# A decay chain behind each projection, a stacked low-rank product, earlier masks and ScalarE evictions in a two-layer backbone step

## The chip, the cores and the metric

The kernel runs on one core of a Trainium2 chip as one program. The metric is the device time of one execution in microseconds; lower is better. The time of a kernel is the median of several executions. One more execution is taken with the hardware profiler, and all rows below are from that one.

## What is computed

One inference step of a backbone with two layers, for 128 context tokens and 1024 latent tokens (1152 columns in all), width 1024, in f32. The change lies in the first (even) layer, ahead of its attention. Cut to what matters:

```
def even_project(h, w_in):                       # h: normalized and modulated tokens
    qa, ka, va, qb, kb, vb, rb, lr = split_cols(h @ w_in, SIZES_EVEN)

def gla_bidir(q, k, v, lr, w_alpha, b_alpha, s0_f, s0_b):
    la = log_sigmoid(einsum('btzr,zrk->btzk', lr, w_alpha) + b_alpha) / 16     # rank 16, two directions
    ...                                          # chunks of 64 tokens
    bcum = cumsum(ac, axis=3)                    # running sum of the log decay inside a chunk
    attn = where(mask, einsum('nbhid,nbhjd->nbhij', q * exp(bcum), k * exp(-bcum)), 0)

def latent_attention(q, k, v, kc, vc, sink): ... # windowed attention with a sink; q and k rotated first
```

So each layer-0 token gets attention queries, keys and values, queries, keys and values of a gated linear attention with four heads, and 32 low-rank numbers `lr`. A product of `lr` with `w_alpha`, a log-sigmoid and a running sum give one decay array per head, 128 rows (64 forward, 64 backward) by 1152 columns.

## The kernel before

Everything is held transposed: features on the 128 partitions, tokens along the free dimension, in three chunks of 384 columns (`CW`, `NCH`). Products are made at f32 accuracy from rounded halves: `hi` is the value rounded to f32r, `lo` the rest, and `mm3` (lines 147 to 150) issues hi*hi, hi*lo and lo*hi, three passes of TensorE. A plain f32 product is issued as two passes.

SBUF is cut into one-buffer slots, `us(i)` (lines 84 to 90): a tile named for slot i takes the slot when the earlier tile of that slot has been read for the last time. Slots 32 and 33 are two halves of one double tile (`up(32)`). PSUM has three `mm` banks (`mmps`, line 105), two `S`, two `X` and one `O` (`aux`). Small rings of SBUF buffers hold temporaries: `t` (5), `ta` (3), `raw` (3) and `w` (4, two weight pairs). The order of instructions on each engine is set when the kernel is built: a planner takes, in a simulated run, the instruction that comes first in the program among those that are ready. A later line can therefore run ahead of an earlier one.

The stages around the change, in program order:

- Slots 16 to 23 hold the input X[0] to X[7]. The first chunk is normalized into the halves H (slots 0 to 15).
- **The token-row product** (lines 605 to 623). For each of nine blocks of 128 tokens and for two column halves, 24 passes give 128 tokens by 272 columns: values `vb` of the linear attention (512 columns in all) and, at the end of the second half, the 32 columns of `lr`. The second and third chunk are normalized in between, at blocks 2 and 5 (line 607), in place in X. Each result leaves PSUM by a copy into a `ta` buffer (line 620, ScalarE for the first half and VectorE for the second), is stored to `d_vb`, and the 32 columns are copied to `lrs3` (line 623, VectorE, slot 32).
- Nine transposes and three copies turn `lrs3` into `lrt`, 32 rows by 1152 (lines 625 to 631, slot 33). `RM` (slot 23) is a mask of ones with a zero at each chunk start; `walp` (slot 22) holds the low-rank weights.
- **gla_pre(hd)** (lines 641 to 655), called for the four heads one after the other: the low-rank product in three chunks (line 647, f32, 32 rows deep), a copy with bias into `et` (line 648, ScalarE), minimum (649), Exp (650), Ln (651), subtraction (652) and the two running sums as scans (653, 654) into `bt`, which goes to `d_b` in DRAM. `et` is slot 31, `bt` slot 30. This is called a decay chain below.
- **Projections.** `proj` takes one weight unit over three chunks, 24 passes each: keys KA (unit 4), rotated by `rope` (lines 664 to 670: a shuffle, two products, one on GpSimd, and a sum); values VST (unit 5); the cached and own keys and values are split into halves; then queries 0 to 3 (lines 720 to 724), each evicted by ScalarE (line 674), rotated and stored to `d_qa`.
- Nine attention blocks, a further projection and two modulation units (`ada_unit`) between each, and behind the last block `gla_init`, which loads the masks `mq` and `m2` (lines 855 to 858), and `gla_a(0)`. Then the linear attention, the output projection, the feed-forward part and the second layer. None of these is edited except `gla_init`.

## Time and profile before

| | us |
|---|---|
| median of 3 runs | 2837.32 (2836.78 to 2839.9) |
| profiled execution | 2838.03 |
| its span, first to last instruction | 2836.3 |
| TensorE busy | 2685.5 (95%) |
| VectorE busy | 2056.6 (73%) |
| ScalarE busy | 1310.2 (46%) |
| GpSimd busy | 1321.5 (47%) |
| mean granted TensorE clock | 0.960 |

PE is TensorE, PEld its weight loads, DVE VectorE, ACT ScalarE, POOL GpSimd, SP SyncE. A busy share is an average over the whole span; for one stage the tables by stage count. The granted clock is the part of 2.4 GHz that TensorE had; 0.50 is its lower level of 1.2 GHz. A wait is put down to what ended last before the engine went on. The end of a matmul is modelled, so neighbouring passes overlap in the rows: the distance of their starts is their cost. Lines 139, 140, 144, 145 and 148 to 150 are helpers that many stages use.

### The profile page before, as it was taken

The numbers are of one execution on the slowest core, as the hardware profiler recorded it, in microseconds if no ns is written. First come the engines' busy times: TensorE is split into PE (matmuls) and PEld (weight loads), VectorE is DVE, ScalarE is ACT, GpSimd is POOL, SyncE is SP. The second block draws the span as 40 slices with busy tenths as digits, with TensorE's granted clock in tenths as the row PEclk, the third lists the DMA queues.
The fourth block names the chain that finished last, engine by engine and source line by source line (L and its number), as shares of the span: only waits on it lengthen the run. The fifth ranks groups of instructions, "written<-read, shape, count | busy, mean of one in ns | idle before, by whom it ended". The sixth has DMA issues, their size and how long they took to land. (4 is left out here: it accounts for less than half of the span.)

```text
span 2836.3 us, 48190 instructions
## 1 busy us (share of the span) xinstructions
PE 2685.5 (95%) x18540; PEld 2549.1 (90%) x18540; DVE 2056.6 (73%) x3544; ACT 1310.2 (46%) x2369; POOL 1321.5 (47%) x783
## 2 busy tenths in 40 slices
PE   6999996888999999999999899989899999999998
PEld 4888884666999999999999899989899999999998
DVE  5466667653588878778777768866888787778876
ACT  5345556434543444435334365564634434443433
POOL 4230104322565555456555536543555555455453
PEclk8999997879999999999999999999999999999999
DMA  8125347643153222622323223453433224433322
GB/s 283 58 85 175 125 140 248 196 147 123 61 208 97 83 90 86 229 88 85 102 83 116 73 75 125 137 164 105 160 131 92 89 89 129 156 96 106 99 83 71
DMA packets 134661, 346.55 MB, mean 122 GB/s; under 512 B 14336, under 2 KB 60416, under 8 KB 134432
## 3 DMA queue, kind: packets, MB, share of 16 engines
q1 hardware_dynamic: 134432, 343.48, 37.1%
q8 instruction: 146, 2.39, 0.3%
q14 instruction: 83, 0.68, 0.1%
HBM read 282.66 MB, written 60.76 MB: 121 GB/s over the span
## 5 line engine op out<-in xcount | busy, mean ns | idle before, releaser
L150 PE MATMUL mm<-u,w 128*128 128x384 f32 (+1 forms) x1324 | 423.9, 322 | 4.2 <-POOL w L140 4.2
L148 PE MATMUL mm<-u,w 128*128 128x384 f32 (+1 forms) x1241 | 401.4, 324 | 4.7 <-DMA u<-d_yg 3.1
L149 PE MATMUL mm<-u,w 128*128 128x384 f32 (+1 forms) x1241 | 398.7, 322 | 3.2 <-POOL u L145 3.2
L140 POOL TENSOR_TENSOR w<-raw,w 128x1024 fp32r<-128x1024 f32 (+1 forms) x67 | 149.1, 2226 | 359.6 <-ACT w L139 299.8
L150 PEld LDWEIGHTS mm<-u,w 128*128 128x128 f32 x1324 | 252.9, 191 | 9.1 <-POOL w L140 4.7
L148 PEld LDWEIGHTS mm<-u,w 128*128 128x128 f32 x1241 | 238.1, 192 | 13.7 <-issue 9.0
L149 PEld LDWEIGHTS mm<-u,w 128*128 128x128 f32 x1241 | 238.1, 192 | 4.9 <-POOL u L145 3.4
L317 DVE SCALAR_TENSOR_TENSOR u<-mm,mods,u 128x288 f32<-128x288 f32 (+4 forms) x345 | 145.4, 451 | 86.2 <-PE mm L150 79.6
L150 PE MATMUL mm<-u,u 128*128 128x288 f32 (+1 forms) x672 | 198.4, 297 | 0.2 <-POOL u L445 0.2
L150 PE MATMUL X<-u,w 128*128 128x288 f32 (+1 forms) x644 | 196.7, 307 | 0.0
L148 PE MATMUL mm<-u,u 128*128 128x288 f32 (+1 forms) x606 | 180.3, 298 | 5.5 <-ACT u L394 3.7
L149 PE MATMUL mm<-u,u 128*128 128x288 f32 (+1 forms) x606 | 180.0, 297 | 0.4 <-POOL u L395 0.3
L148 PE MATMUL X<-u,w 128*128 128x288 f32 (+1 forms) x577 | 175.1, 305 | 2.4 <-DVE u L145 2.4
L149 PE MATMUL X<-u,w 128*128 128x288 f32 (+1 forms) x577 | 175.2, 304 | 1.1 <-DVE u L278 1.1
L148 PE MATMUL S<-u,w 128*128 128x288 f32 (+1 forms) x526 | 161.8, 308 | 10.0 <-ACT t L1178 3.8
L149 PE MATMUL S<-u,w 128*128 128x288 f32 (+1 forms) x526 | 161.1, 306 | 3.0 <-DVE u L1149 3.0
L148 PE MATMUL mm<-u,c 128*128 128x288 f32 (+2 forms) x497 | 153.1, 308 | 0.7 <-DVE ta L505 0.7
L149 PE MATMUL mm<-u,c 128*128 128x288 f32 (+2 forms) x497 | 152.0, 306 | 0.0
L451 POOL TENSOR_TENSOR u<-raw 128x512 f32<-128x512 f32 x82 | 135.8, 1656 | 32.6 <-DMA raw<-in_w_fi_dram 16.4
L447 DVE TENSOR_TENSOR u<-u,raw 128x512 f32<-128x512 f32 x82 | 142.0, 1731 | 0.8
L148 PE MATMUL X<-u,u 128*128 128x288 f32 x433 | 128.6, 297 | 1.5 <-ACT u L449 0.6
L149 PE MATMUL X<-u,u 128*128 128x288 f32 x433 | 128.3, 296 | 0.2
(450 smaller groups left out, 9133.6 us busy)
## 6 DMA issues: line engine op xcount, KB each, us to landing
raw<-in_w_fi_dram SPq DMA_DIRECT2D x164, 512.0 KB, 3.6
raw<-in_w_fo_dram SPq DMA_DIRECT2D x96, 384.0 KB, 3.1
raw<-in_w_ada_dram SPq DMA_DIRECT2D x48, 512.0 KB, 4.8
c<-in_w_ada_dram SPq DMA_DIRECT2D x32, 512.0 KB, 5.4
d_w<-u SPq DMA_DIRECT2D x20, 512.0 KB, 3.6
u<-d_w SPq DMA_DIRECT2D x20, 512.0 KB, 4.9
u<-in_w_ada_dram SPq DMA_DIRECT2D x16, 512.0 KB, 10.3
raw<-in_w_fo_dram SPq DMA_DIRECT2D x16, 512.0 KB, 4.1
```

Source lines behind the costliest of these rows:

```text
L140: gp.tensor_tensor(out=lo[:, :n], in0=raw[:, :n], in1=f_(hi[:, :n]), op=ALU.subtract)
L148: pe.matmul(ps, wh, hh, start=first, stop=False)
L149: pe.matmul(ps, wh, hl, start=False, stop=False)
L150: pe.matmul(ps, wl, hh, start=False, stop=last)
L317: ve.scalar_tensor_tensor(x, ps[:, s0:s1], mod(l, j, cond, n), x, op0=ALU.mult, op1=ALU.add)
L447: ve.tensor_tensor(out=s2, in0=s1, in1=a11, op=ALU.subtract)
L451: gp.tensor_tensor(out=s3, in0=a11, in1=a21, op=ALU.subtract)
```

## The change

1. `lrs3` moves from slot 32 to slot 21. Both halves of each token-row result, and the 32 columns, are copied out by ScalarE.
2. `lrt` becomes an f32r tile of 96 rows in the left half of the double slot 32: rows 0 to 31 and 32 to 63 the rounded half, written by two ScalarE copies, rows 64 to 95 the rest, by one VectorE subtraction. `walp` is stacked to match (rounded, rest, rounded), made from the loaded weights `wa` (slot 20). Line 647 becomes one f32r product 96 rows deep, the sum of the three partial products.
3. The four chains are no longer called in a row: `gla_pre(0)` follows the key projection, `gla_pre(1)` to `gla_pre(3)` follow the projections of queries 0 to 2. Queries 0 and 1 are projected, rotated and stored ahead of the splits of keys and values, query 2 is projected ahead of them and rotated behind them, query 3 stays behind. The slots of the query tiles change accordingly (21, 28, 21, 22).
4. The load and the two copies of the masks move from `gla_init` to ahead of the rotation tables.

```diff
-        lrs3 = us(32)[:, :288].rearrange("p (b n) -> p b n", b=9)
+        lrs3 = us(21)[:, :288].rearrange("p (b n) -> p b n", b=9)
...
-                (sc.copy if hf == 0 else ve.tensor_copy)(s, ps[:, :n])
+                sc.copy(s, ps[:, :n])
                 sy.dma_start(out=d_vb[blk][:, hf * 272:hf * 272 + n], in_=s)
                 if hf == 1:
-                    ve.tensor_copy(lrs3[:, blk], ps[:, 240:272])
-
-        lrt = us(33)[0:32]
+                    sc.copy(lrs3[:, blk], ps[:, 240:272])
+
+        lrt = up(32, F32R)[:, :U]
         for b0, b1 in ((0, 4), (4, 8), (8, 9)):
...
-            ve.tensor_copy(lrt[:, b0 * 128:b1 * 128], ps[0:32, :n])
+            g = slice(b0 * 128, b1 * 128)
+            for q in range(2):
+                sc.copy(lrt[q * 32:q * 32 + 32, g], ps[0:32, :n])
+            ve.tensor_tensor(out=lrt[64:96, g], in0=ps[0:32, :n], in1=f_(lrt[0:32, g]), op=ALU.subtract)
...
-        walp = us(22)[0:32, :512].rearrange("p (h n) -> p h n", h=4)
-        sy.dma_start(out=walp, in_=A["w_alp"])
+        walp = us(22, F32R)[:, :512]
+        wa = us(20)[0:32, :512]
+        sy.dma_start(out=wa.rearrange("p (h n) -> p h n", h=4), in_=A["w_alp"])
+        for q in range(2):
+            sc.copy(walp[q * 64:q * 64 + 32], wa)
+        ve.tensor_tensor(out=walp[32:64], in0=wa, in1=f_(walp[0:32]), op=ALU.subtract)
...
-                pe.matmul(ps[:, :CW], walp[:, hd], lrt[:, ch(c)], start=True, stop=True)
+                pe.matmul(ps[:, :CW], walp[0:96, hd * 128:hd * 128 + 128], lrt[0:96, ch(c)], start=True, stop=True)
...
-        for hd in range(4):
-            gla_pre(hd)
-
+        mqf = tmpa(384)
+        sy.dma_start(out=mqf, in_=A["gmask"])
+        ve.tensor_copy(mq.rearrange("p a b -> p (a b)"), mqf[:, :256])
+        ve.tensor_copy(m2, mqf[:, 256:])
...
-        KA, VST = us(18), us(20)
+        KA = us(18)
         proj(wload(A["w_ef"][4]), H, ev_to(KA))
+        gla_pre(0)
+        VST = us(20)
...
         VA = [us(28, F32R), us(29, F32R)]
+        for j in range(2):
+            q = us(21 if j == 0 else 28)
+            proj(wload(A["w_ef"][j]), H, ev_to(q))
+            gla_pre(j + 1)
+            rope(q)
+            sy.dma_start(out=d_qa[j], in_=q)
+        q2 = us(21)
+        proj(wload(A["w_ef"][2]), H, ev_to(q2))
+        gla_pre(3)
         SM = us(30, F32R)
...
-        for j in range(4):
-            q = us(21 + j % 2)
-            proj(wload(A["w_ef"][j]), H, ev_to(q))
+        for j in range(2, 4):
+            q = q2
+            if j == 3:
+                q = us(22)
+                proj(wload(A["w_ef"][j]), H, ev_to(q))
             rope(q)
             sy.dma_start(out=d_qa[j], in_=q)
...
         def gla_init():
-            mqf = tmpa(384)
-            sy.dma_start(out=mqf, in_=A["gmask"])
-            ve.tensor_copy(mq.rearrange("p a b -> p (a b)"), mqf[:, :256])
-            ve.tensor_copy(m2, mqf[:, 256:])
             t = us(12)
```

## Rows read from the trace of the kernel before

**Rows 1.** The page, its first part: busy us, share of span, instructions.
```profile
PE 2685.5 (95%) x18540; PEld 2549.1 (90%) x18540; DVE 2056.6 (73%) x3544; ACT 1310.2 (46%) x2369; POOL 1321.5 (47%) x783
```

**Rows 2.** Stages of 10 us: length, busy us by engine (instructions), PEclk, DMA, GB/s.
```profile
60.00:70.00 10.00, 8.95 (x71) 8.73 (x70) 9.79 (x18) 6.06 (x12) 9.78 (x8) 1.00 0.34 120
...
130.00:140.00 10.00, 8.58 (x26) 6.41 (x25) 7.68 (x7) 3.89 (x6) 3.40 (x1) 0.69 0.38 119
...
150.00:160.00 10.00, 6.42 (x26) 4.23 (x24) 6.98 (x3) 2.66 (x5) 1.42 (x1) 0.88 0.33 113
160.00:170.00 10.00, 10.00 (x42) 8.87 (x42) 5.15 (x5) 5.66 (x6) 3.38 (x2) 0.78 0.00 1
```

**Rows 3.** List of waits, 60 to 260 us: us in total, times, longest.
```profile
ACT u L648 <- DVE u L654: 22.7, 3, 9.2
...
PE S L647 <- ACT u L648: 5.4, 3, 3.6
```

**Rows 4.** Timeline of PE: start us, us, instruction, [idle before <- releaser].
```profile
68.47 0.40 PE L616 MATMUL mm<-u,u 128*128 128x272 f32 x1 [1.05 <-DVE u L278]
...
80.32 0.83 PE L239 MATMUL S<-ident,r 128*128 128x128 f32 x6
...
110.41 0.91 PE L647 MATMUL S<-u,u 32*128 32x384 f32 x2
111.24 0.45 PE L148 MATMUL mm<-u,w 128*128 128x384 f32 x1
111.53 0.34 PE L149 MATMUL mm<-u,w 128*128 128x384 f32 x1
111.70 0.35 PE L150 MATMUL mm<-u,w 128*128 128x384 f32 x1
...
132.60 0.91 PE L647 MATMUL S<-u,u 32*128 32x384 f32 x2 [1.42 <-ACT u L648]
```

**Rows 5.** Timeline of DVE, columns as in rows 4.
```profile
67.17 0.78 DVE L254 TENSOR_TENSOR t<-t 128x384 f32<-128x384 f32 x1
...
127.36 4.58 DVE L654 TENSOR_TENSOR_SCAN u<-u,u 64x1152 f32<-64x1152 f32 x1
...
478.52 0.22 DVE L858 COPY m<-ta 128x128 f32<-128x128 f32 x1
482.91 0.64 DVE L928 COPY u<-S 64x256 f32<-64x256 f32 x1 [4.17 <-ACT u L928]
```

**Rows 6.** Timeline of ACT, 117 to 133 us.
```profile
117.11 0.58 ACT L648 ACTIVATE u<-S,cols 128x384 f32<-128x384 f32 x1 [1.16 <-PE S L647]
...
131.97 1.05 ACT L648 ACTIVATE u<-S,cols 128x384 f32<-128x384 f32 x2 [6.61 <-DVE u L654]
132.91 0.48 ACT L674 COPY u<-mm 128x384 f32<-128x384 f32 x1
```

**Rows 7.** Lines 623, 639, 655: duration ns min/median/max, first and last start us.
```profile
L623 DVE COPY u<-mm x9: 173/178/181, 57.0 to 106.4; 128x32 f32<-128x32 f32 x9
...
L639 SPq EVENT_SEMAPHORE  x1: 1447/1447/1447, 88.1 to 88.1; - x1
...
L655 SPq DMA_DIRECT2D d_b<-u x4: 319/320/320, 132.0 to 196.0; - x4
```

**Rows 8.** Timeline of ACT, 55 to 90 us.
```profile
55.33 0.26 ACT L231 ACTIVATE r<-S,epst 128x3 f32<-128x3 f32 x1 [1.14 <-PE S L229]
...
57.37 0.48 ACT L260 COPY t<-S 128x384 f32<-128x384 f32 x1
...
88.33 0.68 ACT L275 ACTIVATE S<-u,mods 128x384 f32<-128x384 f32 x1 [0.57 <-DVE u L278]
88.95 0.70 ACT L272 ACTIVATE u<-u,mods 128x384 fp32r<-128x384 f32 x1
```

**Rows 9.** Timeline of POOL: normalization of the second and third chunk.
```profile
59.75 10.03 POOL L267 TENSOR_TENSOR u<-u,t 128x384 f32<-128x384 f32 x8
81.74 7.84 POOL L267 TENSOR_TENSOR u<-u,t 128x384 f32<-128x384 f32 x8 [11.97 <-ACT t L260]
```

## The prediction, made before the changed kernel was run

> **What bounds the kernel now.** I read the page first: TensorE is busy for 95% of the span [rows 1], so time is won where TensorE waits, runs at the lower clock, or has fewer passes to run. The tables by stage come next. The change touches the stretch from 57 us (first blocks of the token-row product) to the end of the key and query projections, and the masks, which are used after 478 us. From 60 us on the token-row product feeds TensorE almost without a gap (8.95 of 10 us, clock 1.00). The projections don't: 8.58 busy at clock 0.69, then 6.42 at 0.88 [rows 2]. The list of waits says why: TensorE's product of line 647 waits for ScalarE's line 648 (5.4 us in three waits), and line 648 waits for the scan of line 654 (22.7 us in three waits) [rows 3]. The four decay chains share one pair of tiles, `et` and `bt`, so that one chain can't write `et` before the chain ahead of it has scanned. The chain shows in the timelines: line 648 ends its three pieces at 117.7 us, the second scan ends at 131.94 us, and only then ScalarE starts the next chain at 131.97 us; an eviction of a projection, due earlier, goes out behind it at 132.91 us [rows 5, 6]. TensorE's share of this is the 1.42 us ahead of its pass at 132.60 us [rows 4].
>
> The price of such a gap is more than the gap: the granted clock falls behind it. Over 10 us, 0.69 means 3.1 us lost against 1.00; the windows behind the second gap lose 1.2 and 2.2 us, 3.4 together [rows 2]. The two levels are 1.2 and 2.4 GHz, so each gap buys some 6 to 7 us at the lower one. The chains thus cost TensorE 5.4 + 3.1 + 3.4 = 11.9 us.
>
> **The stacked product.** A pair of f32 passes of line 647 takes from 110.41 to the next pass at 111.24 us, 0.83 us; the rounded f32 passes beside it start 0.17 us apart (111.53 and 111.70) [rows 4]. Twelve pairs are 10.0 us; twelve single passes of 384 columns over 96 rows are 2.1 us. The trace has no 96-row pass; the nearest rows are these two, and I take the lower one, as type and columns are the same. This is work of a TensorE that is the bound: **-7.9 us**, at least 0 and at most that. What it adds (six copies and three subtractions for `lrt`, two copies and one subtraction for `walp`, one more load) is under 0.7 us each by the copies of the neighbouring rows, on ScalarE and VectorE. It is hidden by the first projection, 72 passes x 0.17 = 12.2 us, which needs none of it; uncovered it would cost about 3 us.
>
> **One chain behind each projection.** A chain takes 117.11 to 131.94 us after its third piece, 14.8 us, plus 1.9 for the pieces, so 16.7 us [rows 5, 6]. The distance of the stores of the chains is now (196.0 - 132.0) / 3 = 21.3 us [rows 7]. A projection and its passes of line 647 are 12.2 + 0.5 = 12.7 us of TensorE. After the change the first chain has two projections behind it and is done in time; the second and third still overrun theirs by up to 4.0 us, so two of the three waits can come back. I take half of the 11.9 us as won, **-6 us**, with the ends 0 and -12. The rotation of q adds its vector work between the chains as now; the loads of rotation tables, caches and weights keep their place in the queue of SyncE, but the stores of `d_b` now come one per projection, in front of `d_qa`, not ahead of all.
>
> **Evictions on ScalarE, and the new slot of `lrs3`.** Taken by itself the move is cheap: nine copies of 0.18 us [rows 7] and the nine larger ones beside them leave VectorE, which is full in the 60 to 70 us window, 9.79 of 10 us, and go to ScalarE with 6.06 [rows 2]. But `lrs3` also moves from slot 32 to slot 21, and slot 21 holds X[5], which the third chunk's normalization reads until 89.0 us (88.33 + 0.68) [rows 8]. Does a tile wait for the whole of the earlier one? Yes: `walp` fills columns 0 to 511 of slot 22, the third chunk's read of X[6] touches columns 768 to 1151 only, and yet SyncE sat 1447 ns at line 639 until 89.6 us, when that read ended (88.95 + 0.70) [rows 7, 8]. So the first copy into `lrs3` now has to wait for X[5]; before, it ran at 57.0 us [rows 7]. Until it has run, the bank of its product isn't free, and there are three `mm` banks: blocks 0, 1 and 2 each leave one occupied, and TensorE stops behind the first chunk. No other work can take its place, since the projections and the modulation products use the same three banks.
>
> When does X[5] come free with TensorE stopped? The sum of squares of the third chunk ends at 67.95 us [rows 5], and the small products that follow, now behind other blocks, come at once: 1.14 + (57.85 - 55.33) = 3.7 us by the second chunk's rows [rows 8], so 71.6 us; GpSimd is done with the second chunk at 69.8 us and needs 7.84 / 8 = 0.98 us for each k [rows 9], six of them to 77.5 us; ScalarE read X[5] 1.4 us behind that (89.0 against 81.74 + 5.88), so 78.9 us, and 79.1 with the copy. Block 3 starts there and not at 68.47 us [rows 4]: 10.6 us. Off go the 0.8 us of the products of line 239, which now lie in the gap [rows 4], on go 3.2 us for the clock as behind the gaps above: **+13.0 us**. Ends: +8 (the clock doesn't fall, and the sums come 2 us earlier as VectorE has fewer evictions ahead of them), and +24 if X[5] comes free at 89.0 us as now (89.2 - 68.5 + 3.2).
>
> By the Trainium skill, Perfetto Trace Analysis, Optimization Strategy, the same gap repeating on the engine that should be full can mean that SBUF or PSUM ran out for the next tile; no row of this trace shows it for the `mm` banks in this stretch.
>
> **Masks early.** The load moves in SyncE's queue from behind the attention blocks to ahead of the two rotation tables, where it takes a `ta` buffer for one landing time; the first projection covers it. Two copies leave the later stage on VectorE; the second ends at 478.74 us, and VectorE then idles 4.17 us for something else [rows 5]. Nothing hangs on them: I take the two copies themselves, **-0.5 us**; the ends are -4.2 if the scan that follows moves up by that idle time, and as much the other way if the order around it gets worse.
>
> **Sum.** -7.9 - 6 + 13.0 - 0.5 = -1.4 us. The profiled execution took 2838.03 us for a span of 2836.3, 0.7 us over the median of the runs (2837.32). So 2838.0 - 1.4 = 2836.6 us, and the median would stand near 2836. The order of each engine's instructions is fixed by a planner when the kernel is built, so later stages may come out in another order; I allow 4 us either way for that.
>
> **Rivals.**
> - *The slot doesn't stop TensorE for long*, because the blocks are ordered so that the banks come free, or the third normalization is done much earlier. For it: SyncE, GpSimd and ScalarE all have slack there. Against: three banks and the rows of `walp` [rows 7, 8]. Then -7.9 - 6 to -12 and at most +3: -11 to -20, 2822 us.
> - *X[5] stays late* (slower). ScalarE is now the only engine that empties the banks and also makes half of the normalization. A copy that waits for X[5] stops all that is queued behind it on ScalarE, as line 648 did to the eviction at 132.91 us [rows 6]. If third-chunk work stands behind such copies, X[5] comes free near 89 us: +24 - 14.4 = +10, 2848 us. It decides as soon as X[5] is free after about 85 us. The Trainium skill (PSUM, Engine vs sequencer instructions) states that the queues of ScalarE, VectorE and GpSimd are strictly first in, first out; the trace agrees at 132.91 us, and by that rule this rival holds, with its 2848 us.
> - *The last chain is late.* Counted from the first projection, the second to fourth chains start at 37, 54 and 70 us at 16.7 us each and the last ends at 87; the q projections end at 6 x 12.2 + 2.1 = 75, the next projection fills TensorE to 87. Attention needs the tiles of the last chain (`SM` and its own q tile share slots 30 and 31). At today's distance of 21.3 us the last chain ends at 37 + 3 x 21.3 = 101: up to 14 us of waiting, of which later projections fill about half: -1 + 7 = +6, 2844 us.
>
> **How the numbers follow.** About 0.2% (5.7 us) is what a measurement of this kernel can tell from no change. The forecast (-12 to +6 around 2836.6) has 0.46, of it 0.35 within 0.2%, 0.07 faster, 0.04 slower. The first rival has 0.28, of it 0.27 faster, 0.01 the same; the second 0.17, of it 0.15 slower and 0.02 the same; the third 0.09, 0.05 slower and 0.04 the same. Faster 0.34, same 0.42, slower 0.24. The range runs from the middle of the first rival's to the second's: 2820 to 2848; the forecast's own is 2825 to 2843.
>
> **What would show it.** Right: a gap of TensorE of about 10 us behind block 2 near 69 us, ended by ScalarE's copy of line 623 or by GpSimd's normalization, with the granted clock at 0.5 after it; single passes of line 647 of 0.17 us pitch; at most two short waits of line 647 for line 648; the time from the first pass of the projections to the last of the fourth query projection down by about 14 us. Wrong: no gap near 69 us, or one of 20 us; or waits for line 654 as long as now. The prediction falls if later stages, above all the stretch after 430 us, move by more than 5 us.

## The result, and the profile after

The changed kernel takes 2857.73 us (median of four runs, 2854.6 to 2862.56) against 2837.07 us before (2836.78 to 2839.9) on the same chip: ratio 1.0084, interval 1.007 to 1.0099. It is slower by some 20 us. The forecast of 2836.6 us was wrong, and so was its range. The profiled execution took 2862.56 us for a span of 2860.8; stage by stage below it is set against the profiled execution of before (2838.03 us).

TensorE is busy for about as long as before [rows 1], with twelve passes less, in a span that is 24.5 us longer. The page's first part, columns as there:

```profile
PE 2675.9 (94%) x18528; PEld 2548.3 (89%) x18528; DVE 2051.8 (72%) x3527; ACT 1315.8 (46%) x2394; POOL 1322.2 (46%) x783
```

In the changed kernel's numbering the copy of the logits is line 623 still, the stacked product is 654 (was 647), the copy into `et` 655 (648), the chain's steps 656 to 661 (649 to 654), the store of `d_b` 662 (655), the rotation 675 to 678 (667 to 670).

I cut the span at five points that both traces have: the last pass of the token-row product, the first score of attention, the first scan of the later stage, the first weight load of the feed-forward part, and the last store. Time from one to the next, in us:

| stretch | before | after | difference | predicted |
|---|---|---|---|---|
| start to last token-row pass | 105.7 | 124.3 | +18.6 | +13.0 |
| to the first score of attention | 117.7 | 116.2 | -1.5 | -13.9 |
| to the first scan | 260.2 | 253.9 | -6.3 | 0 |
| to the first feed-forward weights | 212.5 | 222.5 | +10.0 | -0.5 |
| to the last store | 2131.2 | 2134.8 | +3.6 | 0 |
| sum | 2827.3 | 2851.7 | +24.4 | -1.4 |

Two of these points, the first score and the first scan, move against the work around them when the planner changes the order. The last product of attention is a better mark: between the last token-row pass and it both traces have the same 336 passes of each of lines 148, 149 and 150. By it the stretches are:

| stretch | before | after | difference | predicted |
|---|---|---|---|---|
| last token-row pass to last product of attention | 363.8 | 352.8 | -11.0 | -13.9 |
| to the first feed-forward weights | 226.6 | 239.8 | +13.2 | -0.5 |

PE before, then after; the first row of each pair is the last first pass (line 148) of the sixth projection, the second the last product of attention:

```profile
205.99 0.33 PE L148 MATMUL mm<-u,w 128*128 128x384 f32 x1
...
469.47 0.40 PE L827 MATMUL O<-u,u 128*128 128x512 f32 x1
```
```profile
214.21 0.33 PE L148 MATMUL mm<-u,w 128*128 128x384 f32 x1
...
477.08 0.63 PE L848 MATMUL O<-u,u 128*128 128x512 f32 x1
```

So the slot loses 18.6 us, the projections and attention win 11.0 of it back, and 13.2 us go behind attention.

**The first stretch** holds the stop that was predicted. Timeline of the changed kernel, PE:

```profile
70.77 0.29 PE L617 MATMUL mm<-u,u 128*128 128x272 f32 x1
73.77 1.11 PE L229 MATMUL S<-ones,t 128*128 128x1 f32 x6 [2.70 <-DVE u L278]
75.44 1.65 PE L239 MATMUL S<-ident,r 128*128 128x128 f32 x6 [0.56 <-DVE r L232]
85.38 0.59 PE L615 MATMUL mm<-u,u 128*128 128x272 f32 x1 [8.30 <-ACT u L623]
```

Then ACT, DVE and POOL of the same stretch:

```profile
83.96 0.68 ACT L275 ACTIVATE S<-u,mods 128x384 f32<-128x384 f32 x1 [0.37 <-DVE u L278]
...
85.17 0.33 ACT L623 COPY u<-mm 128x32 f32<-128x32 f32 x3
```
```profile
72.69 1.02 DVE L278 TENSOR_TENSOR u<-S,u 128x384 fp32r<-128x384 f32 x2 [0.34 <-ACT u L272]
```
```profile
60.47 9.97 POOL L267 TENSOR_TENSOR u<-u,t 128x384 f32<-128x384 f32 x8
77.67 7.68 POOL L267 TENSOR_TENSOR u<-u,t 128x384 f32<-128x384 f32 x8 [7.23 <-ACT t L260]
```

Read from the bottom. GpSimd is done with the second chunk at 70.4 us and starts the third only at 77.67, 7.23 us later. What it waits for starts with the product of line 229, which could have run at 71.1 us, where TensorE's passes end; it waits 2.70 us for line 278 of VectorE, the last step of the second chunk's normalization, which holds the `S` bank that line 229 wants. ScalarE's read of X[5] ends at 84.64 us, the three copies into slot 21 start at 85.17, and block 3 begins at 85.38 us. In the kernel before block 3 began at 68.47 us [rows 4].

The windows of 10 us show the price (us of the window, PE busy, PEld, DVE, ACT, POOL, PEclk, DMA, GB/s):

```profile
60.00:70.00 10.00, 6.86 (x45) 6.64 (x44) 9.69 (x13) 5.71 (x13) 10.00 (x9) 0.87 0.31 107
70.00:80.00 10.00, 3.82 (x18) 3.21 (x16) 4.98 (x10) 5.71 (x12) 2.77 (x4) 0.67 0.04 12
80.00:90.00 10.00, 4.62 (x20) 4.62 (x21) 6.38 (x12) 7.37 (x16) 6.66 (x9) 0.50 0.34 114
```

TensorE is busy for 6.86, 3.82 and 4.62 us, and the granted clock falls from 0.87 over 0.67 to 0.50, the lower level (1.2 GHz).

**The second stretch** should have brought 13.9 us. By the rows above, the sixth projection ends 89.9 us behind the last token-row pass and not 100.3, so the projections are 10.4 us shorter; but the first score comes only 1.5 us earlier. What stands between them is the last chain. DVE of the changed kernel from the third chain to the fourth:

```profile
185.62 1.32 DVE L675 STREAM_SHUFFLE u<-u 128x1024 f32<-128x1024 f32 x1
186.98 1.23 DVE L676 TENSOR_TENSOR u<-u,u 128x1024 f32<-128x1024 f32 x1
190.47 1.23 DVE L678 TENSOR_TENSOR u<-u,u 128x1024 f32<-128x1024 f32 x1 [2.26 <-POOL u L677]
191.61 1.35 DVE L656 SCALAR_TENSOR_TENSOR u<-u 128x1152 f32<-128x1152 f32 x1
196.67 1.36 DVE L659 SCALAR_TENSOR_TENSOR u<-u,u 128x1152 f32<-128x1152 f32 x1 [3.71 <-ACT u L658]
198.07 4.63 DVE L660 TENSOR_TENSOR_SCAN u<-u,u 64x1152 f32<-64x1152 f32 x1
202.71 2.56 DVE L661 TENSOR_TENSOR_SCAN u<-u,u 64x1152 f32<-64x1152 f32 x1
```

From the rotation's first step to the end of the scans it is 19.7 us, for a projection that takes TensorE some 13. The rotation stands ahead of the chain's first step in VectorE's queue: 1.32 + 1.23 + 2.26 + 1.23 = 6.0 us. The first scan takes 4.63 us, the second 2.56. TensorE waits for the chains as before [rows 3], and once more for VectorE, which empties a projection (line 865) only behind the last chain and its rotation. List of waits, 126 to 260 us, PE (total, times, longest):

```profile
PE S L654 <- ACT u L655: 7.0, 2, 4.3
PE mm L192 <- DVE t L865: 4.9, 1, 4.9
```

The last chain holds what follows: the `SM` tile has `bt`'s slot and waits for the last store (ACT):

```profile
228.58 0.30 ACT L144 CAST u<-ta 128x128 fp32r<-128x128 f32 x1 [8.89 <-DMA d_b<-u]
```

**Behind attention** VectorE works in another order. Before, the first two copies through the mask (line 965, `COPY_PREDICATED`) run ahead of the second head's scans, and TensorE's second group of masked products follows them 37.2 us behind the last product of attention (DVE, then PE):

```profile
505.87 0.73 DVE L965 COPY_PREDICATED u<-mq,X 128x512 f32<-128x512 uint8 x1
...
508.17 3.64 DVE L942 TENSOR_TENSOR_SCAN u<-u,u 64x1152 f32<-64x1152 f32 x1
```
```profile
506.65 2.07 PE L962 MATMUL X<-u,u 64*128 64x128 f32 x8 [2.38 <-DVE u L965]
```

In the changed kernel these scans come first, 12.5 us of them, and the second group starts 45.0 us behind the last product of attention:

```profile
508.73 6.15 DVE L959 TENSOR_TENSOR_SCAN u<-u,u 64x1152 f32<-64x1152 f32 x2
514.89 6.39 DVE L960 TENSOR_TENSOR_SCAN u<-u,u 64x1152 f32<-64x1152 f32 x2
521.32 0.74 DVE L982 COPY_PREDICATED u<-mq,X 128x512 f32<-128x512 uint8 x1
```
```profile
522.11 2.08 PE L979 MATMUL X<-u,u 64*128 64x128 f32 x8 [4.87 <-DVE u L982]
```

That is 7.8 of the 13.2 us at this place. How much of it lasts to the feed-forward part is not shown by this alone: e8 and e15 below have the same order (43.7 us) and still reach the first feed-forward weights 224.5 and 224.9 us behind attention.

### The profile page after: what moved, and what is told of

The parts are those of the page before. It is cut to its first block, busy times and chain, and to the rows that moved or that the text cites. A ratio compares the mean times of both kernels' runs of the same rounds, so it can differ in the third digit from the quotient of the medians.

```text
span 2860.8 us, 48190 instructions
## 1 busy us (share of the span) xinstructions
PE 2675.9 (94%) x18528; PEld 2548.3 (89%) x18528; DVE 2051.8 (72%) x3527; ACT 1315.8 (46%) x2394; POOL 1322.2 (46%) x783
```

## The experiments

My theory after the first look: (T1) the slot of the logits is nearly the whole loss, and the part that was mis-sized in it is the wait for the `S` bank; (T2) the stacked product and the moved chains bring little because the chain on VectorE and ScalarE, not TensorE, sets the pace of the projections. Rivals: the chains behind the projections are the loss; or the loss is made after 480 us. All kernels compute the whole reference, and nothing is left out of any. Ratios are against the kernel before, timed on the same chip beside each group of runs (medians of before: 2833.16 for the first four, 2835.68 for the next four, 2835.82, then 2832.89), with their intervals. Traces of different runs can come from different chips; some 4 us between them mean little. Each trace is one execution, up to 5.4 us off the median of its kernel, and the rest, in which nothing was changed, runs from 2135.5 to 2148.2 us.

All in one table (us from the start of the span; "scans" is the stretch from the first scan to the first feed-forward weights, with TensorE's mean granted clock in it; "attention" is the start of its last product; "rest" is what the span has behind the first feed-forward weights):

| kernel | last token-row pass | last `d_b` store | first score | attention | first scan | scans | clock | rest | ratio |
|---|---|---|---|---|---|---|---|---|---|
| before | 105.7 | 196.0 | 223.4 | 469.5 | 483.6 | 212.5 | 0.80 | 2140.2 | 1 |
| after | 124.3 | 225.2 | 240.5 | 477.1 | 494.4 | 222.5 | 0.79 | 2143.9 | 1.0084 |
| e1 before, slot | 123.6 | 214.6 | 242.2 | 487.8 | 501.9 | 207.7 | 0.87 | 2141.0 | 1.0080 |
| e2 after, slot back | 107.4 | 207.7 | 223.1 | 461.1 | 477.5 | 215.6 | 0.82 | 2140.2 | 1.0023 |
| e3 before, stacked | 105.1 | 191.1 | 217.9 | 461.2 | 475.3 | 209.6 | 0.83 | 2147.1 | 0.9991 |
| e4 before, chains | 105.1 | 207.5 | 222.3 | 469.4 | 483.5 | 211.3 | 0.85 | 2135.5 | 1.0011 |
| e5 after, X[5] first | 118.4 | 219.3 | 234.6 | 472.1 | 494.7 | 202.0 | 0.82 | 2138.9 | 1.0003 |
| e6 after, other bank | 119.0 | 220.0 | 235.0 | 472.0 | 492.6 | 212.5 | 0.85 | 2139.8 | 1.0053 |
| e7 e2, rotations behind | 108.4 | 206.8 | 221.5 | 476.5 | 484.6 | 216.7 | 0.81 | 2143.8 | 1.0032 |
| e8 before, masks, ScalarE | 107.7 | 199.5 | 226.9 | 472.2 | 486.8 | 209.9 | 0.82 | 2137.5 | 1.0013 |
| e9 e5, rotations, two `bt` | 116.2 | 216.7 | 232.2 | 482.7 | 496.1 | 216.2 | 0.82 | 2141.4 | 1.0085 |
| e10 e3, two `bt` | 105.3 | 193.7 | 218.8 | 465.4 | 479.5 | 206.6 | 0.87 | 2148.2 | 0.9985 |
| e11 after, masks late | 124.3 | 225.3 | 240.5 | 477.8 | 492.9 | 217.1 | 0.81 | 2135.9 | 1.0043 |
| e12 before, X[5] first | 104.3 | 194.6 | 222.2 | 466.5 | 480.6 | 210.5 | 0.83 | 2136.2 | 0.9988 |
| e13 e2, masks late | 107.3 | 207.6 | 223.3 | 460.5 | 476.8 | 214.2 | 0.83 | 2140.4 | 1.0007 |
| e14 before, stacked, X[5] first | 104.9 | 190.9 | 217.5 | 462.9 | 477.0 | 207.0 | 0.87 | 2138.4 | 0.9962 |
| e15 before, masks | 105.3 | 196.7 | 224.1 | 468.2 | 482.8 | 210.3 | 0.84 | 2144.6 | 1.0015 |

### Each part alone

**e1, the slot alone**, on the kernel before:

```diff
-        lrs3 = us(32)[:, :288].rearrange("p (b n) -> p b n", b=9)
+        lrs3 = us(21)[:, :288].rearrange("p (b n) -> p b n", b=9)
...
-        lrt = us(33)[0:32]
+        lrt = up(32)[0:32, :U]
```

> The kernel before with lrs3 alone moved from slot 32 to slot 21 (lrt in its own tile of slot 32); VectorE still empties the second halves. Theory: the token-row product waits for the third chunk's normalization to let go of X[5]; TensorE stands still behind block 2, the last pass of the product comes about 18 us later than 106 us, and the total is 12 to 20 us above before (2849 to 2857 us). Rival (the decay chains set the start of attention, so a late token-row product is hidden by them): under 5 us above before.

Measured 2854.49 us, ratio 1.0080 (1.0065 to 1.0095). The wait is that of the changed kernel, though here VectorE makes the copy (PE):

```profile
85.10 0.57 PE L615 MATMUL mm<-u,u 128*128 128x272 f32 x1 [8.30 <-DVE u L623]
```

The one slot number makes a loss as large as that of the whole change. It is still there, 18.3 us, at the last product of attention (487.8 us, before 469.5).

**e2, the changed kernel with the slot put back:** `lrs3` in slot 32 again; the split product's tile and the first query tiles change places for it.

```diff
-        lrs3 = us(21)[:, :288].rearrange("p (b n) -> p b n", b=9)
+        lrs3 = us(32)[:, :288].rearrange("p (b n) -> p b n", b=9)
...
-        lrt = up(32, F32R)[:, :U]
+        lrt = us(21, F32R)[:, :U]
...
-            q = us(21 if j == 0 else 28)
+            q = us(29 if j == 0 else 28)
...
-        q2 = us(21)
+        q2 = us(33)
```

> The changed kernel with lrs3 back in slot 32, lrt in slot 21 instead, queries 0 to 2 in slots 29, 28 and 33. Theory: the gap at 71 to 85 us goes, and the total falls by 12 to 20 us, to 2838 to 2846 us: the slot alone makes the change slower. Rival (the chains behind the projections cost it, each about 20 us of VectorE against 12.8 us of TensorE): 2850 us or more.

Measured 2840.45 us, ratio 1.0023 (1.0013 to 1.0033). The list of waits of PE, same stretch, has the 8.3 us no longer:

```profile
PE mm L615 <- ACT u L623: 0.2, 1, 0.2
```

The last token-row pass is back at 107.4 us, the first score at 223.1. Three quarters of the loss went (1.0084 to 1.0023). What is left of the change still gains nothing, though it is 8.4 us ahead of before at the last product of attention; the stretch from there to the first feed-forward weights is 5.4 us longer (232.0). The profiled execution is 5.4 us faster than the median, so where the last of it goes does not show.

**e3, the stacked product alone:**

```diff
-                pe.matmul(ps[:, :CW], walp[:, hd], lrt[:, ch(c)], start=True, stop=True)
+                pe.matmul(ps[:, :CW], walp[0:96, hd * 128:hd * 128 + 128], lrt[0:96, ch(c)], start=True, stop=True)
...
-            ve.tensor_copy(lrt[:, b0 * 128:b1 * 128], ps[0:32, :n])
+            g = slice(b0 * 128, b1 * 128)
+            for q in range(2):
+                sc.copy(lrt[q * 32:q * 32 + 32, g], ps[0:32, :n])
+            ve.tensor_tensor(out=lrt[64:96, g], in0=ps[0:32, :n], in1=f_(lrt[0:32, g]), op=ALU.subtract)
```

> The kernel before with the stacked low-rank product alone (lrt in slot 29, the loaded weights in slot 20). The prediction's step: 7.9 us of TensorE passes go, so 2829 us. Rival: the chains on VectorE and ScalarE set the pace of this stretch, TensorE's passes were in its slack, so 2835 to 2838 us.

Measured 2829.85 us, ratio 0.9991 (0.9978 to 1.0004): -2.5 us by the ratio, which is not clear of noise, and -4.3 us by the spans, not -7.9. The passes are as cheap as predicted, 0.18 us from one start to the next (PE):

```profile
110.75 0.34 PE L654 MATMUL S<-u,u 96*128 96x384 f32 x1
110.93 0.34 PE L148 MATMUL mm<-u,w 128*128 128x384 f32 x1
```

Much of what they leave comes back as waiting. List of waits, 60 to 260 us:

```profile
PE S L654 <- ACT u L655: 12.3, 3, 7.4
```

TensorE waits 12.3 us for the chain where it waited 5.4 [rows 3], 6.9 us more. ScalarE waits 21.0 us for the scans, 22.7 before. That is what T2 said, but it is not the whole account. From the last token-row pass to the first score (windows of before, then of e3):

```profile
105.70:223.40 117.70, 109.95 (x575) 97.27 (x573) 70.78 (x59) 49.35 (x72) 33.70 (x11) 0.94 0.25 85
```
```profile
105.10:217.90 112.80, 99.33 (x563) 96.40 (x561) 72.92 (x60) 50.70 (x76) 28.86 (x11) 0.92 0.24 84
```

TensorE is busy for 10.6 us less, and the stretch is 4.9 us shorter. At the last product of attention e3 is 8.3 us ahead (461.2, before 469.5), at the first feed-forward weights 11.2; the rest then takes 6.9 us longer (2147.1 against 2140.2), within what that stretch does from kernel to kernel. So T2 holds for the waits, and fails for the time: up to attention the gain is there.

**e4, the chains behind the projections alone** (product in f32, slot and masks as before):

```diff
-        for hd in range(4):
-            gla_pre(hd)
...
+        gla_pre(0)
...
+            gla_pre(j + 1)
             rope(q)
...
+        gla_pre(3)
```

> The kernel before with the chains moved behind the projections alone (f32 product, lrs3 in slot 32, VectorE empties, masks late). Theory: the first chain starts some 10 us later than now and the chains follow each other every 20 us as before, so the last one ends 10 us later and the total is 5 to 12 us above before (2842 to 2849 us). The prediction's step: half of the waits go, 2831 us.

Measured 2836.29 us, ratio 1.0011 (1.0002 to 1.0021). The last store comes 11.5 us later (207.5), the first score 1.1 us earlier: neither the gain of 6 us nor the loss of 5 to 12 us that I expected. The sixth projection ends 4.5 us earlier, counted from the last token-row pass (95.8 us, before 100.3), but TensorE then waits 5.7 us for VectorE's line 763 ahead of the first score, where it waited 2.4 before, and at the last product of attention nothing is left (469.4 us).

**e8, the masks early and ScalarE alone emptying the product**, on the kernel before:

```diff
-                (sc.copy if hf == 0 else ve.tensor_copy)(s, ps[:, :n])
+                sc.copy(s, ps[:, :n])
...
-                    ve.tensor_copy(lrs3[:, blk], ps[:, 240:272])
+                    sc.copy(lrs3[:, blk], ps[:, 240:272])
...
+        mqf = tmpa(384)
+        sy.dma_start(out=mqf, in_=A["gmask"])
```

> The kernel before with two parts of the change: masks early, and ScalarE alone emptying the token-row product (lrs3 in slot 32). All theories: within 3 us of before; the sums of squares of the third chunk end about 1 us earlier.

Measured 2840.1 us, ratio 1.0013 (1.0004 to 1.0022): +3.7 us, of which 2.0 are there at the last token-row pass; within 3 us was expected, and sums of squares that end 1 us earlier (they end 0.5 us later, at 68.45). Those 2 us belong to ScalarE alone emptying the product, as e2 and e13 (107.4 and 107.3 us) have them too, and e15, with the masks alone, does not (105.3).

### What was mis-sized in the slot's term

**e5, X[5] first in the third chunk's normalization**, in the changed kernel. The products are made in the order 5, 0, 1, 2, 3, 4, 6, 7, so X[5] is free five steps earlier:

```diff
-            for k in range(8):
+            for k in order:
...
-                norm(0, 0, X, H, 1 if blk == 2 else 2, inplace=True)
+                norm(0, 0, X, H, 1 if blk == 2 else 2, inplace=True, order=range(8) if blk == 2 else (5, 0, 1, 2, 3, 4, 6, 7))
```

> The changed kernel with the third chunk normalized in the order k = 5, 0, 1, 2, 3, 4, 6, 7. Theory: the wait behind block 2 ends with the last read of X[5], so GpSimd's five products ahead of it (0.96 us each) drop out: the wait of TensorE for line 623 shrinks from 8.3 us to about 3.5, the token-row product ends about 5 us before 124 us, and the total falls by about 5 us against the changed kernel. Rival (the wait ends with the whole normalization, or with ScalarE's queue): no change.

Measured 2837.04 us, ratio 1.0003 (0.9993 to 1.0012). PE and ACT:

```profile
79.58 0.60 PE L615 MATMUL mm<-u,u 128*128 128x272 f32 x1 [2.56 <-ACT u L623]
```
```profile
78.64 0.67 ACT L275 ACTIVATE S<-u,mods 128x384 f32<-128x384 f32 x1 [1.10 <-POOL u L267]
79.34 0.36 ACT L623 COPY u<-mm 128x32 f32<-128x32 f32 x3
```

Block 3 starts 5.8 us earlier, 0.24 us behind the copy, which comes right behind the read of X[5]. So it is X[5] alone that TensorE waited for, and not the chunk. The last token-row pass moves by 5.9 us, where some 5 were expected, and 5.0 us are still there at the last product of attention. The time falls by 20 us, though, far more than expected. The first scan is no earlier than in the changed kernel (494.7 against 494.4), but that is a change of order: in e5 the first masked products run ahead of it (PE),

```profile
490.46 3.00 PE L979 MATMUL X<-u,u 64*128 64x128 f32 x16 [2.11 <-DVE u L945]
```

and in the changed kernel they start at 507.12 us, behind it. From the last product of attention to the first feed-forward weights e5 takes 224.6 us and not 239.8. It is taken up below.

**e6, another bank for the third chunk's statistics**, in the changed kernel: the products of lines 229 and 239 of that chunk go to the banks of tag `X`, not `S`.

```diff
-        def rstd_of(X, a, w=CW):
-            r, ps = rstd_r(sumsq(X, a, w), D, "S", w)
+        def rstd_of(X, a, w=CW, tag="S"):
+            r, ps = rstd_r(sumsq(X, a, w), D, tag, w)
...
-                norm(0, 0, X, H, 1 if blk == 2 else 2, inplace=True)
+                norm(0, 0, X, H, 1 if blk == 2 else 2, inplace=True, rs=None if blk == 2 else rstd_of(X, 2 * CW, tag="X"))
```

> The changed kernel with the small products of the third chunk's normalization in an X bank, not an S bank. Theory: they waited 2.7 us for the second chunk's normalization to leave its S banks, so X[5] comes free, and the token-row product ends, 2 to 4 us earlier (about 121 us). Rival (they waited for the sums of squares or for GpSimd, busy until 70.4 us): no change.

Measured 2849.92 us, ratio 1.0053 (1.0036 to 1.007). PE, then POOL:

```profile
69.71 0.72 PE L229 MATMUL X<-ones,t 128*128 128x1 f32 x6
...
80.54 0.60 PE L615 MATMUL mm<-u,u 128*128 128x272 f32 x1 [8.60 <-ACT u L623]
```
```profile
72.75 7.68 POOL L267 TENSOR_TENSOR u<-u,t 128x384 f32<-128x384 f32 x8 [3.39 <-ACT t L260]
```

Line 229 runs right behind the last pass, GpSimd starts at 72.75 us and not at 77.67, block 3 at 80.54 and not at 85.38. The `S` bank was worth 4.8 us of the stop, and the last token-row pass moves by 5.3 us, which is what the prediction's term was short of (18.6 - 13.0 = 5.6).

### What sets the pace of the chains

**e7, the rotations behind the next chain's first step.** On the kernel of e2; the order of VectorE's queue is given by hand:

```diff
-            gla_pre(j + 1)
-            rope(q)
+            with tc.issue_after(gla_pre(j + 1).ins):
+                rope(q)
```

> The changed kernel with lrs3 back in slot 32 (as in e2) and each rotation's VectorE work queued behind the first VectorE step of the chain it stands beside. Theory: a chain with its rotation takes 20 us of VectorE's queue because the rotation, with its wait for GpSimd, stands ahead of the chain; behind it, it fills the wait for Exp and Ln, the stores of the chains follow each other every 16 to 17 us and not 20, the last one comes about 10 us earlier than in e2 (197 us, not 208), and the total falls by 4 to 10 us against e2. Rival (the chains are hidden by TensorE's other work): the stores move, the total stays within 3 us of e2.

Measured 2845.33 us, ratio 1.0032 (1.0022 to 1.0042). My theory fell: the stores are 21.1 us apart ((206.8 - 143.5) / 3), not 16 to 17, and the time is no lower than that of e2. From the last token-row pass to the last product of attention it takes 368.1 us, e2 353.7; why attention is so much longer was not followed. A new wait stands where the rotation stood (DVE):

```profile
172.23 1.36 DVE L656 SCALAR_TENSOR_TENSOR u<-u 128x1152 f32<-128x1152 f32 x1 [3.33 <-DMA d_b<-u]
```

The chain's first step writes `bt`, and `bt` is still being stored. e9 and e10 take that away.

**e9, two places for `bt`, rotations behind**, on the kernel of e5:

```diff
-            et, bt = us(31), us(30)
+            et, bt = us(31), us(30 if hd % 2 == 0 else 33)
```

> The changed kernel with X[5] first in the third chunk's normalization, the rotations' VectorE work behind the next chain's first step, and the chain's second working tile in two places (one for even, one for odd heads); the split product's tile is moved for that. Nothing is left out. Theory: a chain could not start on VectorE before the store of the chain ahead had left its one tile (3.3 and 2.9 us of wait in the kernel where only the rotations were moved). With two places the wait for the store is gone: d_b stores 16 to 18 us apart instead of 19 to 21, the last near 210 instead of 219.3, attention's first score near 227 instead of 234.6, and the time some 5 us under that of the kernel with X[5] first alone (so near 2830, ratio 0.998). Rival, VectorE's own busy time and GpSimd beside it set the pace: stores still 19 to 21 us apart, last store within 3 us of 219, time within 4 us of that kernel's.

Measured 2860.81 us, ratio 1.0085 (1.0071 to 1.01). The theory fell again. The rival held for the stores, which are 21.6 us apart ((216.7 - 151.9) / 3), but not for the time, which is some 23 us above that of e5 where it allowed 4: 12.8 us of that come between the last token-row pass and the last product of attention (366.5 against 353.7), and why is not shown. No wait for a store is left. Some of VectorE's steps are stretched (DVE, then POOL):

```profile
170.06 4.74 DVE L661 TENSOR_TENSOR_SCAN u<-u,u 64x1152 f32<-64x1152 f32 x1
```
```profile
169.56 2.83 POOL L140 TENSOR_TENSOR w<-raw,w 128x1024 fp32r<-128x1024 f32 x1 [1.77 <-ACT w L139]
```

A scan that takes 2.55 us takes 4.74 beside GpSimd's product, and a product of the rotation, at 203.58 us, 3.20 in place of 1.23. But e5 has such steps too: four scans of 4.39 to 4.63 us there, five steps of 3.06 to 4.75 here. So this does not explain the pace, which stays open.

**e10, two places for `bt` with the stacked product alone**, on the kernel of e3; the edit of `bt` is that of e9.

> The kernel before with the stacked split product alone, and with two places for the chain's second working tile. Nothing is left out. Theory: in the four chains that follow each other with nothing between, the next one's first VectorE step also waits for the store ahead; with two places it starts while ScalarE and the store are busy, so the four chains shrink from 59.1 us (first to last store 132.0 to 191.1) to some 50, and the time falls by up to 8 us under that of the stacked product alone: 2822 to 2830 (ratio 0.996). Rival: VectorE is in order and already has the scans of the chain ahead in front of it, so nothing overlaps that did not before: last store near 190, time within 3 us of the stacked product's (ratio 0.999).

Measured 2832.16 us, ratio 0.9985 (0.9975 to 0.9995). The rival held: last store at 193.7 us, 191.1 without the second place. The first step of the second chain starts no earlier than without the second place (140.02 us in e3, where it takes 3.45 us); in both it runs beside a product of GpSimd (DVE, then POOL):

```profile
140.31 3.44 DVE L656 SCALAR_TENSOR_TENSOR u<-u 128x1152 f32<-128x1152 f32 x1
```
```profile
139.40 3.12 POOL L140 TENSOR_TENSOR w<-raw,w 128x1024 fp32r<-128x1024 f32 x1 [14.61 <-ACT w L139]
```

### The loss behind attention

**e11, the changed kernel with the masks late again:**

```diff
-        mqf = tmpa(384)
-        sy.dma_start(out=mqf, in_=A["gmask"])
-        ve.tensor_copy(mq.rearrange("p a b -> p (a b)"), mqf[:, :256])
-        ve.tensor_copy(m2, mqf[:, 256:])
...
+            mqf = tmpa(384)
+            sy.dma_start(out=mqf, in_=A["gmask"])
+            ve.tensor_copy(mq.rearrange("p a b -> p (a b)"), mqf[:, :256])
+            ve.tensor_copy(m2, mqf[:, 256:])
```

> The changed kernel with the masks loaded and copied late again, in the stage with the scans, as in the kernel before. Nothing is left out. Theory A, the masks are neutral and the 10 us that the stage with the scans lost come from the order of work that was settled by other edits: time within 4 us of the changed kernel's 2857. Theory B, the early masks cost something of their own (the kernel before with masks early and ScalarE alone emptying the product was 3.6 us slower): the stage from first scan to first weights of the feed-forward part falls from 222.5 to some 212, the time by 4 to 10 us, to 2847 to 2853.

Measured 2848.01 us, ratio 1.0043 (1.003 to 1.0057): 0.41% or some 12 us under the changed kernel by the ratios. Up to the first score the two traces agree; the first scan comes 1.5 us earlier and the feed-forward weights 6.9 us. The other 8.0 of the 14.9 us between the two spans lie in the rest (2135.9 and 2143.9 us). Windows of the changed kernel, then of e11:

```profile
520.00:530.00 10.00, 5.52 (x40) 3.17 (x40) 8.60 (x21) 2.47 (x8) 4.61 (x3) 0.50 0.29 89
530.00:540.00 10.00, 10.00 (x44) 6.64 (x40) 1.33 (x3) 3.53 (x11) 3.63 (x3) 0.50 0.54 190
540.00:550.00 10.00, 10.00 (x56) 6.82 (x54) 1.49 (x8) 0.46 (x2) 3.38 (x4) 0.74 0.63 207
```
```profile
520.00:530.00 10.00, 7.15 (x54) 4.63 (x56) 7.59 (x21) 2.84 (x9) 2.98 (x3) 0.60 0.45 155
530.00:540.00 10.00, 9.65 (x65) 6.33 (x63) 3.89 (x11) 3.40 (x11) 4.07 (x3) 1.00 0.53 187
540.00:550.00 10.00, 10.00 (x62) 7.76 (x62) 3.73 (x7) 2.20 (x9) 2.95 (x3) 1.00 0.50 146
```

TensorE is all but full from 530 us on in both. If the clock rises once in these rows, it does so at 528 us in e11 (0.60 over 520 to 530 us) and at 545 in the changed kernel (0.74 over 540 to 550), which stays at the lower level for 17 us more. In full-speed time that is up to 0.10 x 10 + 0.50 x 10 + 0.26 x 10 = 8.6 us, for a start of the second group of masked products that differs by 1.65 us (520.46 and 522.11 us); the weights come 6.9 us later.

**e12, X[5] first in the kernel before**, where no tile waits for X[5]; the edit is that of e5.

> The kernel before with X[5] first in the third chunk's normalization. Nothing is left out. In this kernel the log-decay logits stay in a slot of their own, so no wait goes with X[5]. Theory: X[5] first helps only where the logits' slot is that of X[5]: the last token-row pass stays within 2 us of 105.7, attention's first score within 2 us of 223.4, and the time within 4 us of before (ratio 0.9986 to 1.0014); whatever of the changed kernel's 20 us came back with X[5] first then came from the slot and what stood behind it. Rival, the order of the eight products is worth something by itself, or the order of later work moves with it: the time differs by more than 5 us.

Measured 2831.27 us, ratio 0.9988 (0.9979 to 0.9998), between the two: 4 us less, without a wait on X[5] that could have gone. The last token-row pass is 1.4 us earlier, the first scan 3.0 (480.6 us), and the scans take 2.0 us less.

**e13, the slot back and the masks late**, the kernel of e2 with the edit of e11.

> The changed kernel with the logits back in the slot of their own and the masks late: what is left of the change is the stacked product, the chains behind the projections and ScalarE alone emptying the product. Nothing is left out. Theory, the early masks cost 4 to 9 us by themselves: 4 to 9 us under the slot-back kernel (which was 1.0023 of before), so 2830 to 2838, ratio 0.999 to 1.001, and the stage from first scan to first feed-forward weights some 5 us shorter than its 215.6. Rival, no cost of their own, only another place in which the clock stays low: within 4 us of the slot-back kernel, ratio 1.001 to 1.0037, and the difference that there is follows the mean granted clock of that stage (0.82 in the slot-back kernel).

Measured 2834.2 us, ratio 1.0007 (0.9996 to 1.0018).

**e15, the masks early alone**, on the kernel before: the edit of e11 the other way round.

> The kernel before with the masks loaded and copied early, nothing else. Nothing is left out. Theory, early masks cost 4 to 9 us by themselves: ratio 1.0015 to 1.003, with the loss between first scan and first feed-forward weights (212.5 in before). Rival, they are neutral but for where the clock stays low: ratio 0.999 to 1.001, nothing up to the first scan at 483.6 moved by more than 2 us.

Measured 2836.33 us, ratio 1.0015 (1.0006 to 1.0023).

The early masks cost 0.16% in e13 against e2, 0.15% in e15, 0.41% in e11 against the changed kernel: the same sign three times, 4 us on two kernels and some 12 on the third. That speaks for a small cost of their own. Its place does not show: e15 is 3.0 us ahead of before at the first feed-forward weights and loses 4.4 in the rest, in an execution that is 3.1 us slower than its median. I found no wait that names the masks. In the changed kernel the clock of e11's windows can account for the 6.9 us at the feed-forward weights; the 8.0 us behind them, and the 4 us, stay without a mechanism.

**e14, the stacked product and X[5] first**, on the kernel before: the edits of e3 and e5.

> The kernel before with the stacked product and X[5] first in the third chunk. Nothing is left out. Theory, the two small gains (ratios 0.9991 and 0.9988) have different places, the chains at 110 to 190 us and the stretch after 480 us, and add up: ratio 0.998, some 2830. Rival, what X[5] first gained was one draw of where the clock stays low after 480 us, and another order draws again: anything from 0.997 to 1.002, with the stage from first scan to first feed-forward weights between 202 and 216 us.

Measured 2821.85 us, ratio 0.9962 (0.995 to 0.9974). It is faster than both kernels, by 0.4 and 1.2%, and the gain is no smaller than the two together (0.9991 x 0.9988 = 0.9979); it lies a little below what theory and rival gave. The last product of attention comes 6.6 us earlier than before (462.9). The last store is at 190.9 us and the first score at 217.5, as with the stacked product alone; the scans take 207.0 us at a clock of 0.87, 2.6 us less than in e3 and 5.5 less than before, so part of the gain may be a good draw of that stretch, as its rival had it.

## Why the prediction was wrong

**The slot: right mechanism, term too small.** The three banks, the whole slot that waits for X[5], the place of the stop and the copy of line 623 that ends it are all there, and e1 and e2 show it from both sides. The prediction said +13.0 us; 18.6 were measured, inside its own ends of +8 and +24. The step that failed is "the small products that follow, now behind other blocks, come at once". They came at 73.77 us, 2.70 us behind the last pass, because they take their bank from the second chunk's normalization; and they ran longer (1.11 and 1.65 us; in e6, 0.72 and 0.94), in a stretch with a granted clock of 0.67. So GpSimd began at 77.67 us and not at 71.6, and X[5] was read at 84.64 and not at 78.9. e6 gives 4.8 us of this back by changing nothing but the bank. The rival in which X[5] stays late set its point at 85 us; the measured 84.64 is all but there, by another road: no third-chunk work stood behind a blocked copy for long, as that rival had it. In e1 VectorE makes the copies, and the gap is the same 8.30 us, so ScalarE's queue did not make it. The Trainium skill (PSUM, Engine vs sequencer instructions) says that ScalarE's queue is strictly first in, first out; no run here speaks against that, but it did not decide.

**The stacked product: right passes, and a gain that does not last.** The pitch was right, 0.18 us. "This is work of a TensorE that is the bound" held in part: TensorE waited there already for the chains [rows 2, 3], and e3 shows 6.9 us more waiting at the same line, against 10.6 us less of busy time. At the last product of attention three kernels with the stacked product and the chains in their old place (e3, e10, e14) are 3.7 to 7.7 us shorter from the last token-row pass on, so most of the 7.9 us can arrive there. The step that failed is the silent one, that what is won there is still won at the end: e3 is 2.5 us faster, not clear of noise.

**The chains: the wrong price of a chain.** The prediction took 16.7 us for a chain and said that the rotation "adds its vector work between the chains as now", without a number. In the changed kernel the rotation takes 6.0 us of VectorE's queue, and one round is 19.7 us (19.65 by its rows) against a projection of 13. So the waits of the stacked product's line were not halved: 7.0 us, where 5.4 stood before. The projections with the stacked product came out 10.4 us shorter, near the 14 that the prediction named as its sign, but the last chain then held up the start of attention. This is the third rival: it said that the last chain ends 101 us after the first projection, and it ended 225.2 - 124.3 = 100.9 us after the last token-row pass (40.1 to the first store and three rounds of 20.3, where the rival had 37 and 21.3). It had a chance of 0.09. Its price of 7 us does not show at the last product of attention, where the whole change is 11.0 us shorter, of 13.9 predicted. In e4 the chains alone bring nothing by that point, where -6 us was predicted. What sets the round is not one wait: with the rotation out of the way (e7) and with the wait for the store gone too (e9), it is still 21.1 and 21.6 us.

**The masks and the emptying by ScalarE: -0.5 us predicted, +4 measured** (e8, e15). The ends of the masks' term, 4.2 us to either side, held it. The emptying, which had no term, takes 1.6 to 2.0 us at the last token-row pass (e2, e8, e13).

**The order of later work: 4 us allowed, 17 found.** This is the largest step that failed: "later stages may come out in another order; I allow 4 us either way for that". The prediction had named its own test, that it falls if later stages move by more than 5 us. From the last product of attention to the first feed-forward weights the changed kernel takes 13.2 us longer, and 3.7 more behind them. It does not look like chance alone: the eight kernels that hold the stacked product, the moved chains and the emptying by ScalarE take 224.6 to 239.8 us for that stretch, 230.8 in the mean, and the other nine 220.7 to 226.6, 223.7 in the mean. The rows of VectorE show one place, the second head's scans ahead of the first copies through the mask, with 7.8 us at the second group of masked products. In e5 the first two of these copies run ahead of all scans, and the second group starts 21.3 us behind the last product of attention, not 45.0: there its 20 us begin. The clock is part of it too: of the seventeen kernels, the four with a mean clock of 0.79 to 0.81 over the scans take 217 us in the mean ((222.5 + 212.5 + 216.7 + 217.1) / 4), the seven of 0.82 and 0.83 take 211, the six of 0.84 and more 209. Why the planner chose the other order, and how much of each part lasts to the end, stays open.

Taken together, by the spans: the slot cost 18.6 us where 13.0 were predicted, the projections and attention won 11.0 of 13.9, and the work behind attention lost 16.9 where -0.5 was predicted and 4 allowed. The slot is shown as the cause of a loss as large as the whole (0.80% alone, 0.61% when it is put back). That the rest of the change gains nothing without the slot is shown by e2; that it wins some 8 us up to attention and loses them behind it is read from the traces, and no run holds the order fixed to prove it.

## What to carry to other kernels

Before a tile is moved to another slot, look up who reads the slot last and how long the banks hold until then: here one slot number cost more than all the rest of the change could win. If the list of waits names another engine at the line whose passes you cut, expect part of the saved time back as waiting there. Follow a gain to the next point that has the same work in both traces: the first instruction of a later stage can move with the order and hide what was won. Price the whole round of an in-order engine (chain, rotation and what runs beside them), not the chain alone, and treat a gain of a few us as real only if it survives a control that changes the order without changing the cause.

## What the runs showed of the hardware

**VectorE beside GpSimd.** A scan, or another step of VectorE that reads two inputs from SBUF, that starts while GpSimd makes a product waits for GpSimd's end, as it seems, and then takes its own time. In the changed kernel the scan starts at 198.07 us and GpSimd's product runs until 197.66 + 2.63 = 200.29:

```profile
197.66 2.63 POOL L140 TENSOR_TENSOR w<-raw,w 128x1024 fp32r<-128x1024 f32 x1 [7.23 <-ACT w L139]
```

That is 2.22 + 2.55 = 4.77 us by this reading, 4.63 measured. In e10 it is 142.52 - 140.31 + 1.36 = 3.57 us, 3.44 measured; in e9 172.39 - 170.06 + 2.55 = 4.88, 4.74 measured. The Trainium skill (Trainium Architecture — The Big Picture, What this means for kernel authors) says that the port pair shared by VectorE and GpSimd is taken by an exclusive lock and not split. These three rows agree with it. Not every step of VectorE is held up: in the changed kernel the rotation's shuffle starts at 139.44 us, beside a product of GpSimd that runs until 139.14 + 2.40 = 141.54, and takes 1.37 us, as long as alone (1.32).

**The clock can decide more than the wait.** The changed kernel and e11 start the same products 1.65 us apart, and by their windows the clock rises 17 us apart. In a stage with many short stops, a change of a microsecond is not paid in microseconds.
